# Two products of a Strassen-Winograd down projection kept in PSUM over six groups, and the activation sums moved from Pool to VectorE

## The chip, the cores and the metric

One core of one Trainium2 chip. The metric is the device time of one execution in microseconds (us), the median of several runs. TensorE (PE in the profile) does the matmuls into PSUM, which has eight banks of 128 partitions x 512 fp32; VectorE (DVE) and ScalarE (ACT) read PSUM and SBUF; Pool (GpSimd) works on SBUF here; SP issues the DMAs.

## The reference, cut to what matters

A trunk of two residual layers on 512 tokens of width 1024 in float32: sparse attention, then gated linear attention, each followed by a LayerNorm and a dense MLP. The MLP is the part that the change touches:

```
def squared_relu_mlp(x, w_up, w_down):          # w_up 1024 x 4096, w_down 4096 x 1024
    return jnp.square(jax.nn.relu(x @ w_up)) @ w_down
h = layer_norm(DN_ALPHA * h + squared_relu_mlp(h, mlp_w_up[i], mlp_w_down[i]), ...)   # twice, i = 0 and 1
```

## The kernel before, in words

Every float32 product is made of three fp32r matmuls (`mm3`, lines 181 to 186): high part times high part, high times low, low times high. So each weight panel is split after its DMA into `w_hi` (a cast on ACT, line 128) and `w_lo` (a subtraction on DVE, line 129), into six buffers of each, and each activation form likewise (`pair`, lines 358 to 364: ACT line 362, DVE line 363).

The MLP (`mlp`, lines 333 to 480) walks over eight groups of 512 hidden features. `up(g)` makes a group of hidden activations: four feature blocks f0 to f3, each 24 matmuls of 512 columns into one PSUM tile of the pool `mm`, then relu on ACT (line 353) and the square on DVE (line 354) into `h2`; the DVE instruction is the last reader of that PSUM bank. `down(g)` multiplies a group with its 512 x 1024 block of `w_down`. For groups 0 to 5 it does so by Strassen-Winograd: the activations are cut in quarters (`a11` ... `a22`), the weights in `b11` ... `b22`, and seven products of half size take the place of eight. `make_forms(g)` builds the sums of activation quarters `s[:,0]` to `s[:,3]` (lines 372 to 375, on Pool) and splits the seven forms; `_load_forms` (lines 144 to 163) builds the four weight sums on Pool (lines 150, 152, 153, 158). Groups 6 and 7 are multiplied plainly at the end (`down_last`).

One product of a down group is done for two token halves j = 0 and 1, two K blocks times three matmuls, so six matmuls per half, each half in a bank of its own. The order in `down` is a11, s2, a12, s1, s3, s4, a22. a12 goes on adding into the banks of a11, and s4 into those of s1, after the first content was read out. After each product DVE adds the bank to a sum in SBUF ("eviction": lines 400, 402, 411, 414, 428; the first group has two copies on ACT in place, lines 409 and 426). `combine` (lines 437 to 445) adds the sums `u2` and `m7` into the residual `xn` on Pool after group 5.

PSUM has eight banks in four pools: `mm` 3 (tiles `ps`), `qk` 2, `po` 1, `tp` 2 (transposes, not used between the first and the last part of the MLP). Before the change `up` uses `mm`; in `down` the banks are a: `qk`, `qk`; b (s2): `mm`, `mm`; d (s1, s4): `mm`, `po`; c (s3): `mm`, `mm`; e (a22): `qk`, `qk`.

The program order is up(0), forms(0), up(1), down(0), forms(1), up(2), down(1), ... The framework plans each engine's instruction order ahead of the run: among the instructions that are ready by its plan it takes the one that stands first in the program. On the chip each engine then goes through its instructions in that fixed order, with semaphores for what they wait for. A weight panel is loaded one panel ahead, so that the splits of a panel stand ahead of the evictions of the group during which they are made.

Of the kernel before, what the change touches and what calls it, by code (L numbers as in the profile page):

```python
# [14 lines left out]
F32 = mybir.dt.float32  # L15
# [5 lines left out]
OP = mybir.AluOpType  # L21
PSUM = bass.MemoryType.PSUM

P = 128
# [6 lines left out]
ALPHA = float((2 * DEPTH) ** 0.25)  # L31
# [61 lines left out]
class Trunk:  # L93
# [239 lines left out]
    def mlp(self, ln_g, ln_b, out):  # L333

        nc, tc = self.nc, self.tc
        G = DFF // 512
        with tc.tile_pool(name="mt", bufs=2) as mt, tc.tile_pool(name="form", bufs=8) as form_p, \
                tc.tile_pool(name="rx", bufs=1) as self.rx, tc.tile_pool(name="gb", bufs=1) as gb_p:
            gb, junk = self.ln_params(gb_p, ln_g, ln_b)
            both = self.big.tile([P, 2, 2, 512], F32, name="big")  # L340
            u2, m7 = both[:, 0], both[:, 1]
            hidden, forms = {}, {}

            def up(g):

                u = self.next_panel()
                h2 = mt.tile([P, 4, SEQ], F32, name="h2")
                step = 256 if g == 0 else 512
                for a in range(0, SEQ, step):
                    for f in range(4):  # L350
                        ps = self.featmajor(u, f * P, P, a, step)
                        r = mt.tile([P, 512], F32, name="relu")
                        nc.scalar.activation(r[:, :step], ps[:, :step], AF.Relu)  # L353
                        nc.vector.scalar_tensor_tensor(h2[:, f, a:a + step], ps[:, :step], 0.0, r[:, :step],  # L354
                                                       op0=OP.max, op1=OP.mult)
                hidden[g] = h2

            def pair(src, n):

                t = form_p.tile([P, 2, 512], F32R, name="form")  # L360
                t = t.rearrange("p c (k s) -> p c k s", k=n)
                nc.scalar.copy(t[:, 0], src)
                nc.vector.tensor_sub(t[:, 1], src, t[:, 0].bitcast(F32))  # L363
                return t

            def make_forms(g):

                h2 = hidden.pop(g)
                a11, a21 = h2[:, 0:2, 0:256], h2[:, 0:2, 256:512]
                a12, a22 = h2[:, 2:4, 0:256], h2[:, 2:4, 256:512]  # L370
                s = self.big.tile([P, 4, 2, 256], F32, name="big")
                nc.gpsimd.tensor_add(s[:, 0], a21, a22)  # L372
                nc.gpsimd.tensor_sub(s[:, 1], s[:, 0], a11)  # L373
                nc.gpsimd.tensor_sub(s[:, 2], a11, a21)
                nc.gpsimd.tensor_sub(s[:, 3], a12, s[:, 1])
                order = (("a11", a11), ("s2", s[:, 1]), ("a12", a12), ("s1", s[:, 0]), ("s3", s[:, 2]), ("s4", s[:, 3]),
                         ("a22", a22))
                forms[g] = {name: pair(x, 2) for name, x in order}

            def product(ps, a, w, j, first=True):  # L380

                tok = slice(j * P, (j + 1) * P)
                for k in range(2):
                    self.mm3(ps, (a[:, 0, k, tok], a[:, 1, k, tok]), (w[0][:, k, :], w[1][:, k, :]),
                             first and k == 0, k == 1, not first)

            def down(g):


                w = self.next_panel()  # L390
                A = forms.pop(g)
                L, R = slice(0, 512), slice(512, 1024)
                xn = self.xn

                def banks(*pools):
                    return [p.tile([P, 512], F32, name=n) for p, n in pools]

                def add(y, ps, op=OP.add):
                    if g == 0:
                        nc.vector.scalar_tensor_tensor(y, y, ALPHA, ps, op0=OP.mult, op1=op)  # L400
                    else:
                        nc.vector.tensor_tensor(y, y, ps, op=op)  # L402

                mm, qk, po = (self.mm, "ps"), (self.qk, "qk"), (self.po, "po")
                a, b = banks(qk, qk), banks(mm, mm)
                for j in range(2):
                    product(a[j], A["a11"], w["b11"], j)
                    if g == 0:
                        nc.scalar.copy(u2[:, j], a[j])
                    else:  # L410
                        nc.vector.tensor_add(u2[:, j], u2[:, j], a[j])
                for j in range(2):
                    product(b[j], A["s2"], w["t2"], j)
                    nc.vector.tensor_add(u2[:, j], u2[:, j], b[j])
                for j in range(2):
                    product(a[j], A["a12"], w["b21"], j, False)
                    add(xn[j][:, L], a[j])
                d = banks(mm, po)
                for j in range(2):
                    product(d[j], A["s1"], w["t1"], j)  # L420
                    add(xn[2 + j][:, R], d[j])
                c = banks(mm, mm)
                for j in range(2):
                    product(c[j], A["s3"], w["t3"], j)
                    if g == 0:
                        nc.scalar.copy(m7[:, j], c[j])
                    else:
                        nc.vector.tensor_add(m7[:, j], m7[:, j], c[j])
                for j in range(2):
                    product(d[j], A["s4"], w["b22"], j, False)  # L430
                    add(xn[j][:, R], d[j])
                e = banks(qk, qk)
                for j in range(2):
                    product(e[j], A["a22"], w["t4"], j)
                    add(xn[2 + j][:, L], e[j], OP.subtract)

            def combine():

                L, R = slice(0, 512), slice(512, 1024)
                add = nc.gpsimd.tensor_add  # L440
                for j in range(2):
                    add(self.xn[j][:, R], self.xn[j][:, R], u2[:, j])
                    add(m7[:, j], m7[:, j], u2[:, j])
                    for c in (L, R):
                        add(self.xn[2 + j][:, c], self.xn[2 + j][:, c], m7[:, j])

            def down_last():

                hs = last.pop(G - 2) + last.pop(G - 1)
                stats = [{} for _ in range(NT)]  # L450
                for half in range(2):
                    u = self.next_panel()
                    for t in range(NT):
                        tok = slice(t * P, (t + 1) * P)
                        y, s, st = self.xn[t], self.sums[t], stats[t]
                        ps = self.mm.tile([P, 512], F32, name="ps")
                        for k in range(8):
                            self.mm3(ps, (hs[k][:, 0, 0, tok], hs[k][:, 1, 0, tok]), u[(k // 4, k % 4)], k == 0, k == 7)
                        self.accumulate(y, s, half, ps, 1.0)
                        self.squares(st, y, s, half, junk)  # L460
                        if half == 1:
                            self.layer_norm(y, s, st, gb[:, 0, :], gb[:, 1, :], None if out is None else out[tok, :])
                            if out is None:
                                self.to_xt(y, t)

            up(0)
            make_forms(0)
            for g in range(1, G - 1):
                up(g)
                down(g - 1)  # L470
                if g < G - 2:
                    make_forms(g)
            combine()
            last = {}
            for g in (G - 2, G - 1):
                if g == G - 1:
                    up(g)
                h2 = hidden.pop(g)
                last[g] = [pair(h2[:, f, None, :], 1) for f in range(4)]
            down_last()  # L480
# [661 lines left out]
```

## Time and profile before

| | |
|---|---|
| median of 3 runs | 1189.71 us (1189.18 to 1190.75) |
| the profiled execution's own time | 1190.91 us |
| span of the profile (first to last instruction) | 1189.1 us |
| mean granted TensorE clock | 0.995 |
| PE busy | 97% |
| DVE busy | 74% |
| ACT busy | 46% |
| Pool busy | 24% |

The busy share of PE is by modelled ends, and matmuls overlap: one of 512 columns is shown as 0.39 us long but the next one starts 0.23 us after it. Gaps are therefore read from start to start: a PE row that shows so much idle time before it started that much plus 0.16 us late. The two MLPs take about 271 to 590 us and 860 to 1189 us of the span.

### The profile page before, as it was taken

To read this page: it belongs to the slowest core of one execution; us is meant where nothing else is said; L and a number is where in the kernel's file an instruction comes from. 1 tells how busy PE (TensorE), PEld (TensorE's weight loads), DVE (VectorE), ACT (ScalarE), POOL (GpSimd) and SP (SyncE) were. 2 spreads that over 40 slices of the span, in tenths; PEclk is the share of its full clock that TensorE was granted. 3 is DMA by queue.
4 is the path that set the end of the run, shared out by engine and by line. 5 is a ranking of instruction groups with operands and counts; after the bars stand their busy time and mean duration, and the time that the engine had idled before them with its cause. 6 is when DMAs were issued, how large, how long until landed. Compare 5 with 4: busy or idle time off the path is not lost.

```text
span 1189.1 us, 15762 instructions
## 1 busy us (share of the span) xinstructions
PE 1156.0 (97%) x5833; PEld 970.8 (82%) x5833; DVE 881.4 (74%) x1615; ACT 547.5 (46%) x933; POOL 289.8 (24%) x192
## 2 busy tenths in 40 slices
PE   8999999999999999999999999999999999999997
PEld 7877888897778778888888998778977788778885
DVE  6899996677787796684754677776687867876746
ACT  6665786534443343343455433344443433453331
POOL 0000000005434325251002345010054252343400
PEclk9999999999999999999999999999999999999999
DMA  5422130421432342253231322032213422432411
GB/s 197 139 72 72 36 107 13 129 72 36 142 106 63 116 142 71 71 177 92 79 112 48 114 88 71 1 118 95 72 54 124 137 73 74 142 93 67 159 36 71
DMA packets 57477, 109.48 MB, mean 92 GB/s; under 512 B 4709, under 2 KB 10089, under 8 KB 57401
## 3 DMA queue, kind: packets, MB, share of 16 engines
q1 hardware_dynamic: 56008, 103.44, 27.6%
q0 software_dynamic: 1392, 5.05, 1.5%
q8 instruction: 46, 0.75, 0.3%
q14 instruction: 31, 0.25, 0.1%
HBM read 106.37 MB, written 2.10 MB: 91 GB/s over the span
## 4 chain that ended last, share of the span: by engine, by line
PE 73%; DVE 13%; issue 5%; POOL 4%; ACT 3%; DMA 0%; SPq 0%; DVEq 0%; ACTq 0%; POOLq 0%
PE ps L184 19%; PE ps L185 19%; PE ps L186 19%; DVE w_lo L129 5%; POOL big L373 2%; PE qk L930 2%; POOL big L372 2%; DVE form L363 1%; PE tps L697 1%; PE tps L226 1%; ACT w_hi L128 1%; PE qk L184 1%; PE qk L186 1%; PE qk L185 1%; DVE big L402 1%
## 5 line engine op out<-in xcount | busy, mean ns | idle before, releaser
L129 DVE TENSOR_TENSOR w_lo<-raw,w_hi 128x1024 fp32r<-128x1024 f32 (+4 forms) x216 | 283.2, 1326 | 31.1 <-ACT w_hi L128 28.9
L128 ACT CAST w_hi<-raw 128x1024 fp32r<-128x1024 f32 (+4 forms) x216 | 219.2, 1022 | 74.1 <-PE ps L185 23.4
L184 PE MATMUL ps<-XT,w_hi 128*128 128x512 f32 (+1 forms) x640 | 236.8, 370 | 4.4 <-DVE h L354 4.4
L185 PE MATMUL ps<-XT,w_hi 128*128 128x512 f32 (+1 forms) x640 | 236.3, 369 | 0.0
L186 PE MATMUL ps<-XT,w_lo 128*128 128x512 f32 (+1 forms) x640 | 236.1, 369 | 0.0
L184 PE MATMUL ps<-w_hi,XT 128*128 128x512 f32 (+5 forms) x440 | 164.7, 375 | 1.3 <-ACT XT L228 0.9
L185 PE MATMUL ps<-w_lo,XT 128*128 128x512 f32 (+5 forms) x440 | 161.8, 368 | 0.2 <-DVE w_lo L129 0.2
L186 PE MATMUL ps<-w_hi,XT 128*128 128x512 f32 (+5 forms) x440 | 161.2, 367 | 0.2 <-DVE XT L229 0.2
L184 PEld LDWEIGHTS ps<-XT,w_hi 128*128 128x128 f32 x640 | 121.0, 189 | 25.7 <-DVE h L354 5.2
L186 PEld LDWEIGHTS ps<-XT,w_lo 128*128 128x128 f32 x640 | 121.1, 189 | 20.4 <-issue 0.2
L185 PEld LDWEIGHTS ps<-XT,w_hi 128*128 128x128 f32 x640 | 121.0, 189 | 20.2 <-issue 0.4
L184 PE MATMUL ps<-w_hi,form 128*128 128x512 f32 x272 | 106.7, 392 | 7.2 <-DVE big L402 4.5
L186 PE MATMUL ps<-w_hi,form 128*128 128x512 f32 x272 | 106.0, 390 | 0.0
L185 PE MATMUL ps<-w_lo,form 128*128 128x512 f32 x272 | 106.0, 390 | 0.0
L184 PEld LDWEIGHTS ps<-w_hi,XT 128*128 128x128 f32 x440 | 83.6, 190 | 12.7 <-ACT XT L228 1.8
L186 PEld LDWEIGHTS ps<-w_hi,XT 128*128 128x128 f32 x440 | 83.5, 190 | 11.3 <-DVE XT L229 0.4
L185 PEld LDWEIGHTS ps<-w_lo,XT 128*128 128x128 f32 x440 | 83.7, 190 | 10.6 <-DVE w_lo L129 0.5
L354 DVE SCALAR_TENSOR_TENSOR h<-ps,relu 128x512 f32<-128x512 f32 (+1 forms) x72 | 44.0, 624 | 45.5 <-ACT relu L353 45.5
L353 ACT ACTIVATE relu<-ps 128x512 f32<-128x512 f32 (+1 forms) x72 | 38.3, 547 | 68.4 <-PE ps L186 61.4
L129 DVE TENSOR_TENSOR w_lo<-t,w_hi 128x1024 fp32r<-128x1024 f32 x12 | 25.7, 2141 | 59.4 <-ACT w_hi L128 59.4
L184 PEld LDWEIGHTS ps<-w_hi,form 128*128 128x128 f32 x272 | 51.0, 188 | 21.5 <-issue 7.6
L150 POOL TENSOR_TENSOR raw<-raw 128x1024 f32<-128x1024 f32 x12 | 29.6, 2467 | 149.3 <-DVE w_lo L129 149.3
(236 smaller groups left out, 2035.1 us busy)
## 6 DMA issues: line engine op xcount, KB each, us to landing
raw<-in_mlp_w_up_dram SPq DMA_DIRECT2D x64, 512.0 KB, 3.9
raw<-in_mlp_w_down_dram SPq DMA_DIRECT2D x64, 512.0 KB, 4.1
raw<-in_b_w_in_dram SPq DMA_DIRECT2D x16, 512.0 KB, 4.6
raw<-in_a_w_in_dram SPq DMA_DIRECT2D x12, 512.0 KB, 4.6
big<-in_x_dram SPq DMA_DIRECT2D x8, 512.0 KB, 4.1
raw<-in_a_w_o_dram SPq DMA_DIRECT2D x8, 512.0 KB, 3.9
raw<-in_b_w_o_dram SPq DMA_DIRECT2D x8, 512.0 KB, 4.7
raw<-in_b_w_in_dram SPq DMA_DIRECT2D x8, 346.0 KB, 4.0
```

The source lines that it names most:

```text
L128: self.nc.scalar.copy(hi, src)
L129: self.nc.vector.tensor_sub(lo, src, hi.bitcast(F32))
L150: sub(t1, b12, b11)
L184: mmul(out, lhs[0], rhs[0], start=first, stop=False, skip_group_check=more)
L185: mmul(out, lhs[0], rhs[1], start=False, stop=False, skip_group_check=more)
L186: mmul(out, lhs[1], rhs[0], start=False, stop=last, skip_group_check=more)
L226: nc.tensor.transpose(tps[:, j, :], src[:, k * P:(k + 1) * P], self.ident)
L353: nc.scalar.activation(r[:, :step], ps[:, :step], AF.Relu)
L354: nc.vector.scalar_tensor_tensor(h2[:, f, a:a + step], ps[:, :step], 0.0, r[:, :step], op0=OP.max, op1=OP.mult)
L372: nc.gpsimd.tensor_add(s[:, 0], a21, a22)
L373: nc.gpsimd.tensor_sub(s[:, 1], s[:, 0], a11)
L930: nc.tensor.matmul(ps[:, h, :], E[:, h, :], E[:, h, :], start=True, stop=True)
```

## The change

In `down`, the product s3 (`m7`) and the product a22 (`m4`) get two banks each for the whole of the six groups: `m7` the two of `qk`, `m4` the two of `tp`. The first group opens the accumulation, the last of the six closes it, and they are not read in between. The products a, b, d share what is left: a `mm`, `mm`; b `mm`, `po`; d `mm`, `po`. `combine` reads `m4` and `m7` once, on DVE. The four sums of activation quarters go to DVE.

```diff
-            both = self.big.tile([P, 2, 2, 512], F32, name="big")
-            u2, m7 = both[:, 0], both[:, 1]
+            u2 = self.big.tile([P, 2, 512], F32, name="big")
+            m7, m4 = [], []
...
-                nc.gpsimd.tensor_add(s[:, 0], a21, a22)
-                nc.gpsimd.tensor_sub(s[:, 1], s[:, 0], a11)
-                nc.gpsimd.tensor_sub(s[:, 2], a11, a21)
-                nc.gpsimd.tensor_sub(s[:, 3], a12, s[:, 1])
+                nc.vector.tensor_add(s[:, 0], a21, a22)
+                nc.vector.tensor_sub(s[:, 1], s[:, 0], a11)
+                nc.vector.tensor_sub(s[:, 2], a11, a21)
+                nc.vector.tensor_sub(s[:, 3], a12, s[:, 1])
...
-                a, b = banks(qk, qk), banks(mm, mm)
+                if g == 0:
+                    m7.extend(banks(qk, qk))
+                    m4.extend(banks(tp, tp))
+                whole = dict(first=g == 0, last=g == G - 3)
+                a, b = banks(mm, mm), banks(mm, po)
...
                 d = banks(mm, po)
...
-                c = banks(mm, mm)
                 for j in range(2):
-                    product(c[j], A["s3"], w["t3"], j)
-                    if g == 0:
-                        nc.scalar.copy(m7[:, j], c[j])
-                    else:
-                        nc.vector.tensor_add(m7[:, j], m7[:, j], c[j])
+                    product(m7[j], A["s3"], w["t3"], j, **whole)
...
-                e = banks(qk, qk)
                 for j in range(2):
-                    product(e[j], A["a22"], w["t4"], j)
-                    add(xn[2 + j][:, L], e[j], OP.subtract)
+                    product(m4[j], A["a22"], w["t4"], j, **whole)
...
             def combine():
                 add = nc.gpsimd.tensor_add
                 for j in range(2):
-                    add(self.xn[j][:, R], self.xn[j][:, R], u2[:, j])
-                    add(m7[:, j], m7[:, j], u2[:, j])
+                    add(xn[j][:, R], xn[j][:, R], u2[:, j])
+                    nc.vector.scalar_tensor_tensor(xn[2 + j][:, L], xn[2 + j][:, L], ALPHA, m4[j],
+                                                   op0=OP.mult, op1=OP.subtract)
+                    nc.vector.tensor_add(u2[:, j], u2[:, j], m7[j])
                     for c in (L, R):
-                        add(self.xn[2 + j][:, c], self.xn[2 + j][:, c], m7[:, j])
+                        add(xn[2 + j][:, c], xn[2 + j][:, c], u2[:, j])
```

## Rows read from the trace of the kernel before

**Rows 1.** The page's first part: busy time, share of the span and instructions of all engines.
```profile
PE 1156.0 (97%) x5833; PEld 970.8 (82%) x5833; DVE 881.4 (74%) x1615; ACT 547.5 (46%) x933; POOL 289.8 (24%) x192
```

**Rows 2.** Busy time by stretch, one round of up(g+1) and down(g): the stretch, its length, then busy us (instructions) of PE, PEld, DVE, ACT, POOL, then the granted clock, the DMA share and GB/s.
```profile
353.00:395.00 42.00, 41.44 (x182) 33.63 (x180) 32.64 (x38) 17.21 (x22) 16.70 (x8) 1.00 0.33 102
```

**Rows 3.** The timeline of PE through one down group (down(1) of the first MLP): start, length, engine, line, operation, out<-in, and in brackets the idle time before it with what ended it.
```profile
339.30 0.39 PE L186 MATMUL ps<-XT,w_lo 128*128 128x512 f32 x1
339.52 0.39 PE L184 MATMUL qk<-w_hi,form 128*128 128x512 f32 x1
...
342.25 0.39 PE L184 MATMUL ps<-w_hi,form 128*128 128x512 f32 x1
...
352.98 0.39 PE L186 MATMUL ps<-w_hi,form 128*128 128x512 f32 x1
353.93 0.47 PE L184 MATMUL ps<-w_hi,form 128*128 128x512 f32 x1 [0.56 <-DVE big L402]
...
359.49 0.39 PE L184 MATMUL ps<-XT,w_hi 128*128 128x512 f32 x1
```

**Rows 4.** The timeline of DVE in the same stretch.
```profile
339.28 4.30 DVE L129 TENSOR_TENSOR w_lo<-raw,w_hi 128x1024 fp32r<-128x1024 f32 x2 [0.19 <-ACT w_hi L128]
343.50 0.68 DVE L354 SCALAR_TENSOR_TENSOR h<-ps,relu 128x512 f32<-128x512 f32 x1
344.11 1.27 DVE L411 TENSOR_TENSOR big<-big,qk 128x512 f32<-128x512 f32 x2
...
348.48 1.23 DVE L363 TENSOR_TENSOR form<-big,form 128x512 fp32r<-128x512 f32 x1 [0.65 <-ACT form L362]
...
350.77 1.27 DVE L402 TENSOR_TENSOR big<-big,qk 128x512 f32<-128x512 f32 x2
351.97 1.21 DVE L129 TENSOR_TENSOR w_lo<-raw,w_hi 128x1024 fp32r<-128x1024 f32 x1
353.11 0.68 DVE L402 TENSOR_TENSOR big<-big,ps 128x512 f32<-128x512 f32 x1
...
354.30 0.68 DVE L363 TENSOR_TENSOR form<-h,form 128x512 fp32r<-128x512 f32 x1
```

**Rows 5.** The timeline of ACT (first row) and POOL (the others) in the same stretch.
```profile
340.45 0.59 ACT L353 ACTIVATE relu<-ps 128x512 f32<-128x512 f32 x1
...
337.87 3.50 POOL L158 TENSOR_TENSOR raw<-t,raw 128x1024 f32<-128x1024 f32 x1 [5.96 <-DVE w_lo L129]
...
344.26 1.29 POOL L372 TENSOR_TENSOR big<-h 128x512 f32<-128x512 f32 x1 [2.90 <-DVE h L354]
345.63 2.16 POOL L373 TENSOR_TENSOR big<-big,h 128x512 f32<-128x512 f32 x1
```

**Rows 6.** The timeline of PE at its four longest waits within the two MLPs: up(1) and down(0) of the first, up(1) and down(0) of the second.
```profile
291.17 0.50 PE L184 MATMUL ps<-XT,w_hi 128*128 128x512 f32 x1 [2.19 <-DVE h L354]
...
312.19 0.50 PE L184 MATMUL ps<-w_hi,form 128*128 128x512 f32 x1 [1.70 <-DVE big L400]
...
880.23 0.62 PE L184 MATMUL ps<-XT,w_hi 128*128 128x512 f32 x1 [2.19 <-DVE h L354]
...
902.17 0.50 PE L184 MATMUL ps<-w_hi,form 128*128 128x512 f32 x1 [1.03 <-DVE big L400]
```

**Rows 7.** Timelines of PE and DVE at three other groups, down(5) and down(0) of the first MLP and down(0) of the second: the first matmul of the product a11, and the DVE instruction that reads f3 last.
```profile
506.41 0.39 PE L184 MATMUL qk<-w_hi,form 128*128 128x512 f32 x1
510.39 0.68 DVE L354 SCALAR_TENSOR_TENSOR h<-ps,relu 128x512 f32<-128x512 f32 x1
...
296.74 0.39 PE L184 MATMUL qk<-w_hi,form 128*128 128x512 f32 x1
301.82 0.68 DVE L354 SCALAR_TENSOR_TENSOR h<-ps,relu 128x512 f32<-128x512 f32 x1
...
887.38 0.39 PE L184 MATMUL qk<-w_hi,form 128*128 128x512 f32 x1
891.81 0.68 DVE L354 SCALAR_TENSOR_TENSOR h<-ps,relu 128x512 f32<-128x512 f32 x1
```

**Rows 8.** The timeline of POOL (three rows) and DVE (two rows) during up(1) of the first MLP, after forms(0) became ready.
```profile
274.25 2.20 POOL L372 TENSOR_TENSOR big<-h 128x512 f32<-128x512 f32 x1 [5.12 <-DVE h L354]
...
279.16 2.85 POOL L150 TENSOR_TENSOR raw<-raw 128x1024 f32<-128x1024 f32 x1
...
298.53 2.28 POOL L374 TENSOR_TENSOR big<-h 128x512 f32<-128x512 f32 x1
...
282.48 6.29 DVE L363 TENSOR_TENSOR form<-big,form 128x512 fp32r<-128x512 f32 x3
...
290.43 1.28 DVE L354 SCALAR_TENSOR_TENSOR h<-ps,relu 128x512 f32<-128x512 f32 x2
```

**Rows 9.** Busy time by stretch right after the third wait of rows 6; the columns are those of rows 2.
```profile
880.20:883.60 3.40, 3.37 (x8) 2.62 (x9) 1.87 (x3) 2.12 (x3) 0.00 (x0) 0.54 0.00 0
```

**Rows 10.** The timeline of POOL and DVE around the combine of the first MLP: the last two Pool additions, and the first DVE instruction of `down_last` that reads `xn`.
```profile
533.28 2.98 POOL L445 TENSOR_TENSOR big<-big 128x512 f32<-128x512 f32 x2
...
552.92 0.69 DVE L269 SCALAR_TENSOR_TENSOR big<-big,ps 128x512 f32<-128x512 f32 x1 [1.37 <-PE ps L186]
```

**Rows 11.** The timeline of PE in `down_last` of the first MLP, where transposes stand between matmuls of one product.
```profile
579.47 0.39 PE L185 MATMUL ps<-w_lo,form 128*128 128x512 f32 x1
579.97 0.41 PE L226 MATMUL tps<-cft,big 128*128 128x128 f32 x2
```

More of the change, by code (lines that the diff above doesn't have):

```diff
@@ L378, in make_forms, with product @@
                 forms[g] = {name: pair(x, 2) for name, x in order}
-            def product(ps, a, w, j, first=True):
+            def product(ps, a, w, j, first=True, last=True, more=False):
                 tok = slice(j * P, (j + 1) * P)
@@ L384, in product @@
                     self.mm3(ps, (a[:, 0, k, tok], a[:, 1, k, tok]), (w[0][:, k, :], w[1][:, k, :]),
-                             first and k == 0, k == 1, not first)
+                             first and k == 0, last and k == 1, more)
             def down(g):
@@ L393, in down, with add @@
                 xn = self.xn
+                mm, qk, po, tp = (self.mm, "ps"), (self.qk, "qk"), (self.po, "po"), (self.tp, "tps")
                 def banks(*pools):
                     return [p.tile([P, 512], F32, name=n) for p, n in pools]
-                def add(y, ps, op=OP.add):
+                def add(y, ps):
                     if g == 0:
-                        nc.vector.scalar_tensor_tensor(y, y, ALPHA, ps, op0=OP.mult, op1=op)
+                        nc.vector.scalar_tensor_tensor(y, y, ALPHA, ps, op0=OP.mult, op1=OP.add)
                     else:
-                        nc.vector.tensor_tensor(y, y, ps, op=op)
-                mm, qk, po = (self.mm, "ps"), (self.qk, "qk"), (self.po, "po")
-                a, b = banks(qk, qk), banks(mm, mm)
+                        nc.vector.tensor_add(y, y, ps)
+                if g == 0:
[3 more added lines that the diff above has]
+                a, b = banks(mm, mm), banks(mm, po)
                 for j in range(2):
@@ L415, in down @@
                 for j in range(2):
-                    product(a[j], A["a12"], w["b21"], j, False)
+                    product(a[j], A["a12"], w["b21"], j, first=False, more=True)
                     add(xn[j][:, L], a[j])
@@ L421, in down @@
                     add(xn[2 + j][:, R], d[j])
-                c = banks(mm, mm)
                 for j in range(2):
-                    product(c[j], A["s3"], w["t3"], j)
-                    if g == 0:
-                        nc.scalar.copy(m7[:, j], c[j])
-                    else:
-                        nc.vector.tensor_add(m7[:, j], m7[:, j], c[j])
+                    product(m7[j], A["s3"], w["t3"], j, **whole)
                 for j in range(2):
-                    product(d[j], A["s4"], w["b22"], j, False)
+                    product(d[j], A["s4"], w["b22"], j, first=False, more=True)
                     add(xn[j][:, R], d[j])
-                e = banks(qk, qk)
                 for j in range(2):
-                    product(e[j], A["a22"], w["t4"], j)
-                    add(xn[2 + j][:, L], e[j], OP.subtract)
+                    product(m4[j], A["a22"], w["t4"], j, **whole)
             def combine():
@@ L440, in combine @@
                 add = nc.gpsimd.tensor_add
+                xn = self.xn
                 for j in range(2):
-                    add(self.xn[j][:, R], self.xn[j][:, R], u2[:, j])
-                    add(m7[:, j], m7[:, j], u2[:, j])
+                    add(xn[j][:, R], xn[j][:, R], u2[:, j])
+                    nc.vector.scalar_tensor_tensor(xn[2 + j][:, L], xn[2 + j][:, L], ALPHA, m4[j],
+                                                   op0=OP.mult, op1=OP.subtract)
+                    nc.vector.tensor_add(u2[:, j], u2[:, j], m7[j])
                     for c in (L, R):
-                        add(self.xn[2 + j][:, c], self.xn[2 + j][:, c], m7[:, j])
+                        add(xn[2 + j][:, c], xn[2 + j][:, c], u2[:, j])
             def down_last():
```

## The prediction, made before the changed kernel ran

> **What bounds the kernel now.** I read the page first: PE is busy 97% of the span, DVE 74%, Pool 24% [rows 1]. Then the busy time by stretch: in a round of up(g+1) and down(g), 42 us long, PE works 41.4 us at full granted clock and DVE 32.6 us [rows 2]. So TensorE sets the time, and another engine counts only where PE stands still for it. The change removes no matmul: what it can win or lose is PE's gaps.
>
> The timeline of PE through one down group shows the cadence. The pair of products a11 starts at 339.52 and the next pair at 342.25: 2.73 us for twelve matmuls, 0.228 us each. Seven pairs end when up begins at 359.49, after 19.97 us; without a gap it would be 7 x 2.73 = 19.1 us. The one gap stands ahead of the pair s4: 352.98 to 353.93 in place of 0.23, so 0.72 us too much, and what ended it is the eviction at line 402 [rows 3].
>
> DVE's timeline beside it says why that eviction is late: two weight splits that take 4.30 us (one alone takes 1.21), then the square of f3, then evictions and further splits without a pause, so that the s1 bank is read at 353.11 to 353.79 only [rows 4]. The split was long because Pool's line 158 ran from 337.87 to 341.37 [rows 5]. Four downs of each MLP have this gap. Beyond them there are four waits: two in up(1), 2.19 us idle each, and two in down(0), 1.70 and 1.03 us [rows 6]; with the 0.16 us by which a shown matmul overlaps the next, 2.35, 2.35, 1.86 and 1.19 us. All gaps of the MLPs together: 8 x 0.72 + 7.75 = 13.5 us, about 1.1%. More than that, and what the clock gives back, can't be won.
>
> **What the change takes away.** In DVE's queue per down group four evictions (s3 and a22), at 0.64 to 0.68 us [rows 4]. In Pool's queue 48 sums, 1.29 to 2.28 us each [rows 5, 8]. In come four sums per group on DVE; the nearest row is an SBUF subtraction of the same size, 0.68 us when Pool is idle [rows 4]. DVE's sum of work stays about even, and since its 32.6 of 42 us are no bound that alone costs nothing: the cover is that forms(g) are needed a whole up later, some 21 us. Dropping the Pool sums also frees the one form that took 1.23 us beside Pool [rows 4]; it is off the path, 0 us. The wait ahead of s4 I expect gone: s4 wants the s1 bank three half pairs, 4.1 us, after it is filled, DVE misses that by 0.72 us only, and the new gap below gives it 2 us more: 8 x -0.72 = **-5.8 us**.
>
> The Trainium skill (Perfetto Trace Analysis, Optimization Strategy) says that the same gap repeating on the engine that should be saturated can mean that PSUM has too few buffers for the next tile. The trace differs here: the gap ends with the reading of a bank that s4 goes on using, not of another tile's. By the page the gap would stay with fewer banks, and the sum below would be 5.8 us higher.
>
> **What it adds: a bank that is not free.** `m7` and `m4` hold four of eight banks; up and down share three of `mm` and one of `po`. Count `mm` at the start of a down: up ended with f1, f2, f3 in its three banks. The pair a11 takes those of f1 and f2, and s2 (j = 0) must have that of f3. Before, s2 had f1's and f2's, a11 had `qk`, and f3's bank was wanted by s1 only, 3 x 2.73 = 8.2 us into the down. Now it is wanted at 2.73 us. When is it free? f3's last matmul starts at 339.30 [rows 3], relu runs on ACT to 341.04 [rows 5], but the square waits in DVE's queue behind the two splits and ends at 344.18 [rows 4], 4.66 us into the down. From the end of a DVE read to the matmul that waited for it the trace has 353.79 to 353.93, 0.14 us [rows 3, 4]. PE would start s2 at 344.32 instead of 342.25: **2.07 us** of gap. The splits stand ahead of the square in program order, and neither they nor line 158 are touched, so this lateness stays; Pool's sums come only after the square and don't make it. Bounds: 0 if other products are put into the gap (first rival), 2.07 if the order stays. I take 2.07, because the order of the products in the trace is the program's.
>
> So the eight downs with the old gap: 8 x (2.07 - 0.72) = **+10.8**. Down(5) has no such gap, but f3's square ends at 511.07, again 4.66 us after 506.41 [rows 7]: 2 x 2.07 = **+4.1**. Down(0) of the first MLP: the square ends 5.76 us in [rows 7], but 1.1 of it is a split that Pool's line 374 held up [rows 8], which goes; 2.07 - 1.86 = **+0.2**. In the second MLP it is 5.11 us, 4.0 without that: 1.4 - 1.19 = **+0.2**.
>
> The second bank: s1 (j = 0) needs one of `mm` when a12 has ended. The bank of s2 (j = 0) is read by then, so 0. If it is given a11's bank, it waits for the eviction of a12 (j = 0), filled 1.36 us before: 0.68, a split of 1.21 ahead of it in the queue, 0.14 and a matmul's 0.16 make 0.8 us. Bounds 0 and 0.8 per down; I take 0.
>
> **up(1).** PE waits there until DVE has squared f0, which stands behind the forms; three of these took 6.29 us while Pool ran lines 150 on [rows 8]. After the change Pool starts its weight sums about 4 us sooner, as its sums are gone (274.25 to 279.16), and DVE does three sums more. Bounds: 0 and -2.35 for each MLP; I take -1.5, since six forms and sums of 0.68 come out of Pool's way: **-3.0 us**.
>
> The Trainium skill (SBUF, Who interferes with whom) says that Pool and a DVE instruction with two SBUF inputs take a port as an exclusive lock and that the loser waits for the whole instruction. The 4.30 us for two splits agree. By it the DVE sums meet Pool's weight sums in up(1), each waits for one, and the 3.0 us are not won.
>
> After the second MLP's up(1) wait the granted clock fell to a mean of 0.54 for 3.4 us, that is to the lower level of 1.2 GHz [rows 9], worth 1.7 us; with a shorter wait I expect it not to fall there: **-1.7 us** (bounds 0 and -1.7).
>
> **combine.** Two Pool additions fewer per MLP, four DVE instructions of 0.68 more. DVE's `u2` + `m7` waits for the Pool addition that reads `u2`; behind it in DVE's queue stand splits and up(7)'s squares, for which PE waits only at its fourth feature block, 16 us into up(7). Before, Pool ended at 536.26 and `xn` was read at 552.92 [rows 10]: cover 16 us, cost 0. Four ACT copies less: 0.
>
> **Sum:** 10.8 + 4.1 + 0.2 + 0.2 - 3.0 - 1.7 = +10.6 us, on the profiled execution's 1190.9 us 1201.5. That execution is 1.2 us above the median of the runs, so 1200.3.
>
> **Rival 1, faster: the order hides the wait.** The planner may see that f3's bank is late and put other ready products between a11 and s2: half of s2 has `po`, s3 has its own banks. It does mix on PE: transposes stand inside a product [rows 11]. From nine matmuls on (2.07 / 0.228) the wait is gone. Then all old gaps go and none comes: -5.8 - 3.0 - 3.0 - 1.7 = -13.5, 1176 us. Against it: at none of the four long waits of rows 6 did it fill the gap; its plan, which orders DVE by readiness, seems not to know Pool's hold on the splits. Chance 0.27.
>
> **Rival 2, much slower.** s1 waits as well, 12 x 0.8 = 9.6 us, and of the twelve new gaps some bring the clock down: one of the four waits of rows 6 did, so three, 5.1 us. Together 1215 us. It decides where s1 gets a11's bank. Chance 0.15.
>
> **Rival 3, nothing.** A few matmuls of s2's other half go ahead (three: 12 x 0.7 us less) and up(1) wins all it can (1.7 more): 1200.3 - 10.1 = 1190. Chance 0.12; the forecast itself 0.46.
>
> **The numbers.** About 0.2%, 2.4 us, can be told from no change. Slower holds the forecast and rival 2, 0.61; rival 3 is the 0.12; faster 0.27. The forecast's own range is 1193 to 1209. For eight in ten I leave out the far half of rivals 1 and 2: 1178 to 1212.
>
> **What would show it.** Right: in each down a PE gap of some 2 us ahead of s2, ended by DVE line 354; none ahead of s4; a DVE queue without evictions behind s3 and a22; Pool's busy time down by some 75 us. Wrong: matmuls into `m7` or `po` between a11 and s2, or the square of f3 ahead of the last split on DVE; and a long wait in up(1) would undo that term.

## The result, and the profile after

The changed kernel takes **1196.08 us** (median of 5 runs, 1195.59 to 1198.23), beside 1190.14 us (1189.18 to 1191.16, 5 runs) for the kernel before on the same chip: the ratio is 1.0054, with a 95% interval of 1.0040 to 1.0069. It is slower, by 5.9 us; the forecast was slower by 10.6. The profiled execution takes 1196.08 us with a span of 1194.3, 5.2 more than the span of before.

The page's first part, and of its costliest groups the one in which each triple of down's matmuls into the `ps` banks begins (busy us, mean ns, then the idle time ahead of them and what ended it):

```profile
PE 1152.4 (96%) x5833; PEld 968.7 (81%) x5833; DVE 879.0 (74%) x1627; ACT 549.1 (46%) x929; POOL 209.4 (18%) x140
...
L184 PE MATMUL ps<-w_hi,form 128*128 128x512 f32 x296 | 116.5, 394 | 19.2 <-DVE h L354 19.2
```

Against [rows 1] Pool has lost 80 us and 52 instructions and DVE 2.4 us. PE does the same number of matmuls and is busy 3.6 us less, yet its span is longer. Every microsecond that these matmuls waited is put down to line 354, the square of the hidden block: 19.2 us, which is 12 x 1.60.

The timeline of PE in down(1) of the first MLP, beside [rows 3]:

```profile
337.05 0.39 PE L186 MATMUL ps<-XT,w_lo 128*128 128x512 f32 x1
337.28 0.39 PE L184 MATMUL ps<-w_hi,form 128*128 128x512 f32 x1
...
340.00 0.39 PE L184 MATMUL po<-w_hi,form 128*128 128x512 f32 x1
341.99 0.50 PE L184 MATMUL ps<-w_hi,form 128*128 128x512 f32 x1 [1.60 <-DVE h L354]
342.33 0.39 PE L185 MATMUL ps<-w_lo,form 128*128 128x512 f32 x1
...
352.55 0.39 PE L186 MATMUL qk<-w_hi,form 128*128 128x512 f32 x1
352.78 0.39 PE L184 MATMUL ps<-w_hi,form 128*128 128x512 f32 x1
...
358.22 0.39 PE L184 MATMUL ps<-XT,w_hi 128*128 128x512 f32 x1
```

Read it by start times. The pair a11 fills 337.28 to 340.00. One single matmul of s2's second half goes into the `po` bank at 340.00, and then PE stands until 341.99: 1.99 us from start to start where 0.23 is usual. The matmul after the wait takes 0.34 instead of 0.23. So a gap costs 1.76 + 0.11 = 1.87 us. All twelve downs show this one, to 0.01 us. At 352.78 s4 follows s3 (the last one into `qk`) without a pause: the old gap is gone. The down group takes 358.22 - 337.28 = 20.94 us, 0.97 more than the 19.97 of before.

DVE and POOL beside it, as in [rows 4, 5]:

```profile
337.03 4.30 DVE L129 TENSOR_TENSOR w_lo<-raw,w_hi 128x1024 fp32r<-128x1024 f32 x2 [0.19 <-ACT w_hi L128]
341.26 0.68 DVE L354 SCALAR_TENSOR_TENSOR h<-ps,relu 128x512 f32<-128x512 f32 x1
341.86 1.27 DVE L415 TENSOR_TENSOR big<-big,ps 128x512 f32<-128x512 f32 x2
...
345.42 0.69 DVE L372 TENSOR_TENSOR big<-h 128x512 f32<-128x512 f32 x1
...
335.62 3.50 POOL L158 TENSOR_TENSOR raw<-t,raw 128x1024 f32<-128x1024 f32 x1 [10.94 <-issue]
```

The two splits still take 4.30 us beside Pool's line 158, the square still ends 4.66 us into the down (341.94 - 337.28), and the first of the sums that came to DVE stands 4 us behind it.

up(1) of the first MLP: DVE after forms(0) became ready, the Pool instruction beside it, and PE's wait, as in [rows 6, 8]:

```profile
275.80 2.77 DVE L373 TENSOR_TENSOR big<-big,h 128x512 f32<-128x512 f32 x1
278.61 2.78 DVE L375 TENSOR_TENSOR big<-h,big 128x512 f32<-128x512 f32 x1
281.31 2.90 DVE L363 TENSOR_TENSOR form<-big,form 128x512 fp32r<-128x512 f32 x1
...
284.73 1.88 DVE L363 TENSOR_TENSOR form<-big,form 128x512 fp32r<-128x512 f32 x3
...
288.28 1.27 DVE L354 SCALAR_TENSOR_TENSOR h<-ps,relu 128x512 f32<-128x512 f32 x2
...
275.30 2.73 POOL L150 TENSOR_TENSOR raw<-raw 128x1024 f32<-128x1024 f32 x1 [56.37 <-DVE w_lo L129]
...
288.45 0.39 PE L186 MATMUL ps<-XT,w_lo 128*128 128x512 f32 x1
289.01 0.50 PE L184 MATMUL ps<-XT,w_hi 128*128 128x512 f32 x1 [0.17 <-DVE h L354]
```

The wait is 0.17 us idle where it was 2.19: with the overlap of shown matmuls and the slow one after it 0.44 in place of 2.46 us, in each MLP.

Two stretches by window, the clock is the number ahead of the last two: after the wait in up(1) of the second MLP, as [rows 9], and a stretch of the mixer between the MLPs. The third row is the same stretch of the mixer in the kernel before, where it comes 3.45 us sooner.

```profile
880.00:883.60 3.60, 3.43 (x15) 2.52 (x15) 2.77 (x5) 2.23 (x4) 0.00 (x0) 1.00 0.00 0
750.45:754.05 3.60, 3.36 (x20) 2.47 (x18) 3.60 (x9) 2.75 (x10) 0.00 (x0) 1.00 0.00 0
```

```profile
747.00:750.60 3.60, 3.60 (x14) 2.64 (x13) 3.60 (x9) 2.29 (x8) 0.00 (x0) 0.55 0.00 0
```

The granted clock is 1.00 in both stretches after, so the run is at 2.4 GHz there; the run of before fell to 1.2 GHz in both. What the stretch in the mixer costs is read from PE's timelines, from the wait ahead of it to the next matmul of 512 columns, before and then after:

```profile
746.38 1.17 PE L930 MATMUL qk<-E 128*128 128x128 f32 x8 [2.06 <-DVE AT L931]
...
751.62 0.48 PE L184 MATMUL ps<-w_hi,XT 128*128 128x512 f32 x1
```

```profile
749.83 1.13 PE L930 MATMUL qk<-E 128*128 128x128 f32 x8 [2.06 <-DVE AT L931]
...
754.04 0.48 PE L184 MATMUL ps<-w_hi,XT 128*128 128x512 f32 x1
```

It is 5.24 us before and 4.21 after, so 1.0 us.

**The budget of the two profiled executions**, from the starts of the same matmuls in both timelines. Each of down(1) to down(4) takes 19.92 to 20.00 us before and 20.94 after, eight times 0.98 = +7.8; down(5) took 19.11 and 19.12, so twice 1.83 = +3.7; down(0) took 21.02 and 20.37 and now takes 20.94 and 20.96, +0.5; up(1), -2 x 2.02 = -4.0; the half clock behind the second up(1) gone, 3.40 us at 0.54 [rows 9], -1.6; that in the mixer gone, -1.0. The sum is +5.4, the executions differ by 5.2.

By the gaps alone each of the eight downs would be 1.07 us longer: 1.87 less the old gap, which is 0.80 (0.72 and 0.08 for the matmul after it). It is 0.98, because something besides the gap went. The pair a12 took 2.79 to 2.86 us before, with no idle time, and takes 2.72 after. In the timeline of [rows 3] a12 and the pair behind it start at:

```profile
344.96 0.42 PE L184 MATMUL qk<-w_hi,form 128*128 128x512 f32 x1
...
347.76 0.39 PE L184 MATMUL ps<-w_hi,form 128*128 128x512 f32 x1
```

### The profile page after: what moved, and what is told of

It reads as the page before. It is cut to its first block, busy times and chain, and to the rows that moved or that the text cites. A ratio compares the mean times of both kernels' runs of the same rounds, so it can differ in the third digit from the quotient of the medians.

```text
span 1194.3 us, 15714 instructions
## 1 busy us (share of the span) xinstructions
PE 1152.4 (96%) x5833; PEld 968.7 (81%) x5833; DVE 879.0 (74%) x1627; ACT 549.1 (46%) x929; POOL 209.4 (18%) x140
## 4 chain that ended last, share of the span: by engine, by line
PE 81%; DVE 11%; issue 4%; ACT 3%; POOL 1%; DMA 0%; SPq 0%; DVEq 0%; ACTq 0%; POOLq 0%
PE ps L184 21%; PE ps L185 20%; PE ps L186 20%; DVE w_lo L129 3%; ACT w_hi L128 2%; PE qk L930 2%; PE tps L226 1%; PE tps L697 1%; PE po L185 1%; PE po L186 1%; PE po L184 1%; PE qk L185 1%; PE tps L185 1%; PE tps L184 1%; PE qk L184 1%
## 5 line engine op out<-in xcount | busy, mean ns | idle before, releaser
L184 PEld LDWEIGHTS ps<-XT,w_hi 128*128 128x128 f32 x640 | 120.7, 189 | 21.5 <-DVE h L354 1.2
L184 PE MATMUL ps<-w_hi,form 128*128 128x512 f32 x296 | 116.5, 394 | 19.2 <-DVE h L354 19.2
L186 PE MATMUL ps<-w_hi,form 128*128 128x512 f32 x296 | 115.4, 390 | 0.0
L185 PE MATMUL ps<-w_lo,form 128*128 128x512 f32 x296 | 115.4, 390 | 0.0
L184 PEld LDWEIGHTS ps<-w_hi,form 128*128 128x128 f32 x296 | 55.6, 188 | 35.4 <-DVE h L354 24.3
```

Of the source, the lines that this page charges most:

```text
L184: mmul(out, lhs[0], rhs[0], start=first, stop=False, skip_group_check=more)
L185: mmul(out, lhs[0], rhs[1], start=False, stop=False, skip_group_check=more)
L186: mmul(out, lhs[1], rhs[0], start=False, stop=last, skip_group_check=more)
```

## The experiments

Theory A: the accumulation costs because it takes banks from a11 and s2, so that s2 wants the bank of f3 before DVE has read it; DVE reads it late because Pool's line 158 holds a split; and the sums on VectorE are a gain of their own. Rivals: the sums lengthen DVE's queue and so make the square late (B); DVE has too much work ahead of the square whatever Pool does (C); four banks are too few for any order (D); accumulating over the groups costs by itself (E). Each kernel was timed in 4 to 6 runs; the kernel before took 1190.12 us beside the first four and 1190.46 beside the last three.

### Accumulation alone: the sums back on Pool

```
-                nc.vector.tensor_add(s[:, 0], a21, a22)      (and the three below it)
+                nc.gpsimd.tensor_add(s[:, 0], a21, a22)
```

> The changed kernel (1196.1 us) with the four sums of activation quarters back on Pool: the accumulation in PSUM alone. Theory A (f3's bank): the wait ahead of s2 does not depend on where the sums run, because they are issued behind f3's square; 12 gaps of 1.87 us again, while up(1)'s wait goes back from 0.44 to 2.35 + 0.11 us twice: +4.0, and +1.7 if the granted clock falls behind it: 1200 to 1202 us. Theory B (DVE's queue, lengthened by the sums, is what makes f3's square late): the gaps ahead of s2 shrink to that of DVE's former load; with 12 x 1.87 = 22.4 us less and 4.0 more it would be about 1178 us.

Measured: 1204.74 us (1202.41 to 1208.49), ratio to before 1.0127 [1.0107, 1.0146]. Theory B falls: ten of the twelve gaps are 1.99 us from start to start again. up(1) waits 2.16 us idle again. I had expected 1200 to 1202; the rest is in PE's longest waits (first fence) and in the windows behind three of them (second, the columns are those of [rows 2]):

```profile
290.49 0.50 PE L184 MATMUL ps<-XT,w_hi 128*128 128x512 f32 x1 [2.16 <-DVE h L354]
302.14 0.50 PE L184 MATMUL ps<-w_hi,form 128*128 128x512 f32 x1 [1.38 <-DVE h L354]
...
885.45 0.80 PE L184 MATMUL ps<-XT,w_hi 128*128 128x512 f32 x1 [2.16 <-DVE h L354]
897.93 0.50 PE L184 MATMUL ps<-w_hi,form 128*128 128x512 f32 x1 [2.20 <-DVE h L354]
```

```profile
291.50:294.90 3.40, 3.40 (x9) 2.67 (x8) 2.52 (x3) 1.88 (x4) 0.27 (x1) 0.50 0.00 0
885.40:888.80 3.40, 3.35 (x8) 2.67 (x9) 1.89 (x3) 1.92 (x3) 0.00 (x0) 0.50 0.00 0
899.10:902.50 3.40, 3.40 (x10) 2.65 (x9) 1.02 (x2) 0.97 (x2) 3.24 (x3) 0.50 0.88 327
```

Three stretches of 3.4 us at clock 0.50 cost some 3 x 1.7 = 5.1 us, where I had allowed for one. So in this execution the sums on Pool cost not only 2.0 us per up(1), but the clock behind the waits as well.

### Sums on VectorE alone: the kernel before with that half of the change

```
-                nc.gpsimd.tensor_add(s[:, 0], a21, a22)      (and the three below it)
+                nc.vector.tensor_add(s[:, 0], a21, a22)
```

> The kernel before (1190.1 us) with the four sums of activation quarters on DVE: the other half alone. Theory A: no bank is wanted earlier, so no gap ahead of s2; up(1)'s wait falls from 2.46 to 0.44 us in each MLP, -4.0 us, the two stretches at half granted clock go or not (0 to -3.4); the eight gaps ahead of s4 (0.8 us) stay, grow or go by where the sums stand in DVE's queue: from -6.4 to 0, as the form of 1.23 us there gives way to a sum of 0.69, I expect them smaller by some 0.5: 8 x 0.5 = 4. In all 1178 to 1186 us, faster. Theory B (DVE's longer queue costs): slower than the kernel before, 1192 or more, with gaps ahead of s2 or s4 grown.

Measured: **1174.58 us** (1173.94 to 1174.91), ratio 0.9868 [0.9855, 0.9882]. This half is a gain of 15.5 us, more than I expected of it, since all eight gaps ahead of s4 are gone, and the two of down(0) too. The group of down's matmuls on the page (no idle time), then the timeline of DVE in down(1) and the first matmul of s4 there:

```profile
L184 PE MATMUL ps<-w_hi,form 128*128 128x512 f32 x272 | 105.8, 389 | 0.0
```

```profile
343.63 0.68 DVE L372 TENSOR_TENSOR big<-h 128x512 f32<-128x512 f32 x1
...
347.70 0.68 DVE L402 TENSOR_TENSOR big<-big,ps 128x512 f32<-128x512 f32 x1
...
349.21 0.39 PE L184 MATMUL ps<-w_hi,form 128*128 128x512 f32 x1
```

The s1 bank is read by 348.38, 12.85 us into the down (which starts at 335.53), and s4 wants it at 13.68. In the kernel before it was read 14.27 us into the down [rows 3, 4]: 1.42 us later. What went is the wait of 0.65 us ahead of the form of 1.23 us and the form itself; a sum of 0.68 has the place.

The two halves do not add up. Accumulation on top of this kernel (that is the changed one) costs 1196.08 - 1174.58 = 21.5 us, close to 12 x 1.87 = 22.4. On top of the kernel before it costs only 1204.74 - 1190.12 = 14.6, as it then closes the old gaps too, which the sums close by themselves: that gain can be had once.

### No Pool work beside these splits: line 158 left out of the changed kernel

```
-        sub(t4, t2, b21)
```

> The changed kernel without line 158: the weight sum t4 = t2 - b21 is not computed (t4 is t2's value), so that Pool no longer runs beside the first split of each down; the output is another. Theory A (f3's square is late because Pool's 3.5 us of line 158 hold DVE's split for 3.16 in place of 1.2 us): the square ends some 1.9 us sooner, at about 2.7 us into the down, just as s2 wants the bank: the gap falls from 1.87 to 0.1 or 0, 12 x 1.8 = 21 us less, 1175 us. Theory C (what is late is DVE's amount of work ahead of the square, Pool has no part in it): gap and time as in the changed kernel, 1196 us.

Measured: 1175.39 us (1174.65 to 1177.78), ratio 0.9879 [0.9866, 0.9893]. Theory C falls. PE and DVE in down(1), which starts at 335.55; lines behind 158 have numbers one lower here:

```profile
338.27 0.39 PE L183 MATMUL po<-w_hi,form 128*128 128x512 f32 x1
338.50 0.49 PE L183 MATMUL ps<-w_hi,form 128*128 128x512 f32 x1
338.83 0.40 PE L184 MATMUL ps<-w_lo,form 128*128 128x512 f32 x1
...
335.31 2.53 DVE L129 TENSOR_TENSOR w_lo<-raw,w_hi 128x1024 fp32r<-128x1024 f32 x2 [0.19 <-ACT w_hi L128]
337.75 0.68 DVE L353 SCALAR_TENSOR_TENSOR h<-ps,relu 128x512 f32<-128x512 f32 x1
```

The two splits take 2.53 us in place of 4.30, the square ends at 338.43, and s2's first half starts at 338.50 with no idle time. The order of the matmuls is that of the changed kernel, the single one into `po` included: that order leaves no gap when nothing holds up DVE. The Trainium skill (SBUF, Who interferes with whom) says that of a GpSimd and a DVE instruction that want the shared port pair one is blocked for the whole of the other. These rows agree: 1.77 us of split go with the one Pool instruction.

### f3's bank wanted half a pair later

```
-                a, b = banks(mm, mm), banks(mm, po)
+                a, b = banks(mm, mm), banks(po, mm)
```

> The changed kernel with the two banks of s2 swapped: s2 (j = 0) goes to the free po bank and s2 (j = 1) to f3's, so that f3's bank is wanted six matmuls (1.36 us) later and the work is the same. Theory A: the gap moves behind the first half of s2 and shrinks from 1.87 to 0.6 us or, as one matmul was put ahead already, by 1.36 - 0.23 = 1.1 us to about 0.7; 12 x 1.1 to 1.3 = 14 to 16 us less: 1180 to 1182 us, faster than both. Theory D (four banks are too few: a bank won here is missed at the next pair): the gap comes back ahead of a12, s1 or s4, about 1190 to 1196 us.

Measured: 1183.39 us (1182.30 to 1185.93), ratio 0.9946 [0.9933, 0.9958]. One line, no work less, and the changed kernel beats the one before. The timeline of PE in down(1):

```profile
343.42 0.39 PE L186 MATMUL po<-w_hi,form 128*128 128x512 f32 x1
344.28 0.50 PE L184 MATMUL ps<-w_hi,form 128*128 128x512 f32 x1 [0.47 <-DVE h L354]
344.62 0.39 PE L185 MATMUL ps<-w_lo,form 128*128 128x512 f32 x1
```

Six matmuls go into `po` first, five more than in the changed kernel; the gap is 0.63 + 0.11 = 0.74 us, 1.13 less, five matmuls of 0.227. 12 x 1.13 = 13.6, and 1196.08 - 13.6 = 1182.5 us. It does not come back at another place, against theory D. (The profiled execution, 1185.93 us, is the longest of the five: from 27.9 to 35.0 us, long before the first MLP, its granted clock was 0.52.)

### f3's bank wanted a whole pair later

```
                 for j in range(2):
+                    product(m7[j], A["s3"], w["t3"], j, **whole)
+                for j in range(2):
                     product(b[j], A["s2"], w["t2"], j)
...
                 for j in range(2):
-                    product(m7[j], A["s3"], w["t3"], j, **whole)
+                    product(m4[j], A["a22"], w["t4"], j, **whole)
...
-                for j in range(2):
-                    product(m4[j], A["a22"], w["t4"], j, **whole)
```

> The changed kernel with its seven pairs of products in another order: a11, s3 (into m7), s2, a12, s1, a22 (into m4), s4. Same banks, same matmuls; s2 wants f3's bank one pair later, 5.45 us into the down, 0.8 us after the square has freed it. Theory A (only the moment at which f3's bank is wanted costs): no gap in any down, 12 x 1.87 = 22.4 us less than the changed kernel: 1173 to 1176 us. Theory D (with four banks held the rest are too few): s4 now follows a22 directly and s2 has less time before a12; gaps come back there, 1180 us or more.

Measured: 1175.46 us (1175.15 to 1175.86), ratio 0.9872 [0.9858, 0.9886]. DVE and PE in down(1), which starts at 335.15:

```profile
339.13 0.68 DVE L354 SCALAR_TENSOR_TENSOR h<-ps,relu 128x512 f32<-128x512 f32 x1
...
340.53 0.39 PE L186 MATMUL qk<-w_hi,form 128*128 128x512 f32 x1
340.76 0.39 PE L184 MATMUL ps<-w_hi,form 128*128 128x512 f32 x1
```

The square is as late as ever, 4.66 us into the down, but s2 now starts at 5.61. With both accumulators, all their four banks and every instruction of the changed kernel in place, 20.6 us go by order alone. A down takes 19.20 to 19.24 us here in place of 20.94, twelve times 1.72. Theory D falls with it.

### One accumulator, the other product read out as before

```
-                    m7.extend(banks(qk, qk))
-                    m4.extend(banks(tp, tp))
+                    m7.extend(banks(tp, tp))
...
-                a, b = banks(mm, mm), banks(mm, po)
+                a, b = banks(qk, qk), banks(mm, mm)
...
-                    product(m4[j], A["a22"], w["t4"], j, **whole)
+                    product(e[j], A["a22"], w["t4"], j)            (e = banks(qk, qk))
+                    add(xn[2 + j][:, L], e[j], OP.subtract)
...                                              (in combine, the instruction that reads m4 goes)
```

> The changed kernel with one product (s3) adding up in PSUM, in the tps banks; a22 is read out in each group as in the kernel before, and a11, s2 and a22 have the banks that they had there, so that f3's bank is wanted by s1 alone, 8.2 us into the down. The sums stay on VectorE. Theory A: no gap ahead of s2 nor s4, 1173 to 1176 us. Theory E (what costs is the accumulation over the groups itself, not the banks that it takes from a11 and s2): half of the 22 us remain, about 1185 us.

Measured: 1174.76 us (1174.30 to 1175.04), ratio 0.9866 [0.9850, 0.9883]: none of the 22 us is left, so accumulating by itself costs nothing (E falls). Nor does it bring anything: the kernel with the sums alone takes 1174.58. Two evictions per group, off DVE's queue, buy no time when PE waits for none of them; nor do the four per group of the run before this one, 1175.46.

### What made the old gap ahead of s4: line 158 left out of the kernel before

```
-        sub(t4, t2, b21)
```

> The kernel before (1190.1 us, sums on Pool, all seven products read out) without line 158, the weight sum t4 (its value is t2's; the output is another). It asks what made the eight gaps ahead of s4. Theory A1 (line 158's hold on the first split, as the prediction had it): DVE is 1.8 us sooner in its queue, the gaps of 0.8 us go, 6.4 us less: 1183 to 1184 us. Theory A2 (the Pool sums of activation quarters, which hold the split to 1.34 and the form to 1.23 us, make it): the Pool sums follow f3's square, which comes 1.8 us sooner as well, so the gaps stay, if smaller: 1188 to 1190 us. The two waits in up(1) stay in both, up to 3.4 us of half granted clock may come or go.

Measured: 1182.13 us (1179.38 to 1183.52), ratio 0.9926 [0.9912, 0.9940]. The gaps ahead of s4 are gone here as well, with the Pool sums in place (A1), and so are those of down(0): each of the twelve downs takes 19.04 us. DVE in down(1), which starts at 341.21, and a row of PE's waits (us in total, times, longest), for line 353, which is line 354 of the others:

```profile
348.40 1.24 DVE L362 TENSOR_TENSOR form<-big,form 128x512 fp32r<-128x512 f32 x1 [0.65 <-ACT form L361]
...
353.03 0.68 DVE L401 TENSOR_TENSOR big<-big,ps 128x512 f32<-128x512 f32 x1
```

```profile
PE ps L183 <- DVE h L353: 4.4, 2, 2.2
```

The form still takes 1.24 us, but s1's bank is read by 353.71, 12.50 us into the down. So the old gap had two causes, and it took both to make DVE miss s4 by 0.72 us: line 158's hold, 1.8 us, and the Pool sums, 1.4 us. Taking either away ends it. The two waits of up(1) remain, as expected.

## Why the prediction was right, and where its sizes were off

The direction was right, and so was the mechanism: the wait ahead of s2 for f3's bank, ended by line 354, in all twelve downs, none ahead of s4, no eviction behind s3 and a22, Pool down by 80 us (75 forecast). That this wait is what makes the change slow is shown by moving only the moment at which the bank is wanted (12.7 and 20.6 us less) and only the moment at which it is free (20.7 us less). Term by term:

| step of the sum | predicted | measured |
|---|---|---|
| eight downs with the old gap | 8 x (2.07 - 0.72) = +10.8 | 8 x (20.94 - 19.96) = +7.8 |
| two downs(5) | +4.1 | 2 x 1.83 = +3.7 |
| two downs(0) | +0.2, +0.2 | 20.94 - 21.02 = -0.1, 20.96 - 20.37 = +0.6 |
| up(1), both MLPs | -3.0 | 2 x (0.44 - 2.46) = -4.0 |
| half clock behind MLP2's up(1) | -1.7 | -1.6 |
| half clock in the mixer | not in the sum | -1.0 |
| second bank (s1), combine | 0, 0 | 0, 0 |
| together | +10.6 | +5.4 |

**The wait, 2.07 us, was mis-sized by 0.20.** "2.07 if the order stays": it did not stay quite. One matmul of s2's other half went ahead, which takes 0.23, and PE followed DVE's read by 0.05 us (341.94 to 341.99), not 0.14; against that the first matmul after a wait costs 0.11 more, which the prediction had counted neither for the new wait nor, with 0.08, for the old gap. This is rival 1's mechanism, one matmul of the nine that it needs. That it is one fits an order laid out for a split that nothing holds, though no run shows the plan itself: the run without line 158 has the same order and no wait. The old downs were also longer than their gaps: 19.97 us against the 19.1 that the prediction worked out is 0.87, of which it explained 0.72. And in the second MLP's down(0) the square is no sooner than elsewhere: it ends 4.66 us into the down, not the 4.0 that the prediction had by taking off the 1.1 us of a split in the first MLP.

**up(1): -1.5 was too little, 2.02 came.** The row on the lock was right in kind: the sums on DVE do meet Pool's weight sums, and two of them take 2.77 us in place of 0.69. By the Trainium skill's rule (SBUF, Who interferes with whom), as the prediction applied it, the gain would be lost there; it was not. By the rows Pool's weight sums start at 275.30 and not at 279.16, DVE's instructions that wait beside them come sooner too, and the squares start at 288.28 where it was 290.43: by these rows what counted was when Pool's run was over, not that the two engines met in it; no run moves the one without the other.

**"It is off the path, 0 us"** was wrong, of the form of 1.23 us that Pool's sum stretched. Sums moved alone end the old gap, so that form, with the wait ahead of it, was on its path: 8 x 0.80 = 6.4 us that the sums' half of the change wins by itself. In the sum it did not show, because the new wait gave s4 the time in any case, as the prediction had it (the run with the accumulation alone has no gap ahead of s4 either), so the total was not hurt; but the split of the change into a good and a bad half, -15.5 and +21.5 us, could not be seen from it. The Trainium skill's rule (Perfetto Trace Analysis, Optimization Strategy), that a repeating gap can mean too few PSUM buffers, was weighed rightly: with four fewer banks free that gap vanished. The new one is of the rule's kind, yet another order of the same products closes it with no bank more, and swapping two banks takes it from 1.87 to 0.74 us.

**The clock.** The stretch behind MLP2's up(1) went as forecast. The stretch of the mixer, 1.0 us, is not shown to be the change's doing. In all nine profiled executions PE waits there 2.06 us for the same DVE instruction (line 931 above); behind it the clock fell in the kernel before and in the two kernels without line 158, and not in the other six. The clock also differs between executions of one kernel: its mean is 0.993 to 0.997 in the twenty runs of the kernel before beside the experiments, and 0.997 or 0.998 in the five of the changed kernel. Rival 2's second half did not happen: of the new waits of 1.60 us none was followed by a lower clock. Its first half, s1 waiting too, did not either.

## What to carry to other kernels

A product kept in PSUM over a loop cost no time here by its adds, but it takes its banks from the rotation, and the next product then wanted a bank that was filled a moment ago: list, for each matmul group, when its bank was last filled and when its reader gets through its own queue, and put the groups that have banks of their own first. An eviction saved on an engine that is not waited for was worth nothing here (two per group, 1174.76 us against 1174.58 without). Measure the two halves of a double change apart, and do not expect them to add up: this one hid 15.5 us of gain behind 21.5 us of loss, where the half that loses costs 14.6 by itself, and swapping two banks gives 12.7 us of the loss back, another order of the products 20.6.

## What the runs showed of the hardware that was not expected

- At full granted clock, the first matmul after each of the changed kernel's twelve waits takes 0.33 or 0.34 us to the next one's start in place of 0.23 (341.99 to 342.33 above). Over twelve waits that is 1.3 us. The wait alone does not make it: in the kernel without line 158 a matmul of 0.33 or 0.34 us stands at the same place of all twelve downs with no idle time ahead of it (338.50 to 338.83 above). What makes it is open.
- Waits inside the MLPs and the clock behind them: of seven waits of 2.16 to 2.20 us idle (two in the kernel before, three in the run with the sums back on Pool, two in the kernel before without line 158) five were followed by 3.4 us at about half clock, each 1.6 to 1.7 us; of the waits of 1.70 us and less (twelve after, eleven with the sums on Pool, ten before, twelve of 0.47 with the banks swapped) none was. The two MLPs of one execution differed in this, so the length of the wait alone does not decide it; the price of one wait in up(1) is 2.5 us or 4.2 by it.
